# The run-up to the first pass of a two-layer decoder trunk: c spread over partitions another way, x in four transfers, the first weights in three pieces

## The chip, the cores and the metric

One core of a Trainium2 chip runs the kernel. The metric is the device time of one execution in microseconds (us), the median over runs.

## What is computed

A trunk of two decoder layers over 256 tokens of width 1024, all in float32. Each layer has a token mixer (layer 0: dilated windowed attention; layer 1: gated linear attention) and a gated convolutional feed-forward part. Each of these four sub-layers is fed a normalised and modulated x; shift, scale and gate come from a conditioning vector c:

```python
mod = jax.nn.silu(c) @ w_ada[i] + b_ada[i]                 # c: (1, 1024), w_ada[i]: (1024, 6*1024)
sh1, sc1, g1, sh2, sc2, g2 = split(mod, 6)
h = rmsnorm(x, norm_mix[i]) * (1.0 + sc1) + sh1            # x: (1, 256, 1024)
y = dilated_mixture(h, w_in_a, w_out_a, rel_bias)          # layer 0; begins with h @ w_in_a
x = x + g1 * y
...
```

`rmsnorm(x, g)` is x / sqrt(mean(x*x) + eps) * g, the mean over the 1024 features.

## The kernel before

x is held transposed: `x_all` is 128 partitions by 8 tiles (`kt`) by 256 tokens, so that a tile `kt` holds 128 of the 1024 features. Products keep float32 accuracy by splitting both operands in a high part (`hi`, in the fp32r format) and a low part (`lo`, what is left): a product is hi*hi + hi*lo + lo*hi.

What lies ahead of the first pass, and the lines that matter:

- **c.** A DMA on ScalarE's queue (line 84) brings c into one partition of `c_row`. Two products with a stationary operand of one row (line 123) spread it over all 128 partitions, ScalarE's Silu (line 124) turns it into `c_bc`. Two more DMAs on that queue bring `small` (biases and norms), `tab` and `oh` (the relative bias table and a one-hot matrix).
- **x.** Two DMAs on SyncE's queue (SP, line 90), 512 KB each.
- **The mean square.** VectorE squares tiles 0 to 3 in one instruction (line 385), ScalarE squares 4 to 7 in two (line 388); VectorE adds each half down to one tile in two sums (line 391); two products with a matrix of 1/1024 (line 211, in `rstd_of`) sum over partitions; Ln and Exp (lines 213 and 215) make `rstd`.
- **Filling products.** `keep_warm` (line 297) issues products whose result nobody reads: 4 behind the products of c, 3 behind the mean square, 6 behind the rows of the bias (line 405), which are themselves three small products of `oh` and `tab`.
- **The first pass**, a loop over the 8 tiles `kt`. For each tile SP loads 1 MB of modulation weights (`ada_load`, line 133) and 960 KB of attention weights (`split`, line 166). VectorE takes two dot products of 1024 columns with `c_bc` (`ada_dot`, line 140); ScalarE adds bias and factor (lines 148 and 150); VectorE forms `xr` (line 283), ScalarE its high part `hhi` (line 285), VectorE the low part `hlo` (line 287). The weight tile is cast to its high part `whi` in two halves of 960 columns on ScalarE (line 172), the low parts `wlo` are VectorE's (line 184). TensorE then multiplies (lines 675 and 679, and 199 to 201 for the rest). For kt = 0 both loads go in two DMAs.

The order of the instructions of an engine follows from a scheduler, with dependences written out by hand: `behind(a, b)` and `issue_after` put an instruction behind others. The weights' raw buffers are four in number (`wraw`), so a load waits until the tile two rounds back has been consumed. Each DMA of SP and ScalarE also waits for the DMA eight places ahead of it among those of these two queues.

## Time and profile before

| | |
|---|---|
| time, median of 3 runs | 765.04 us (764.12 to 766.68) |
| the profiled execution: time, span | 764.38 us, 762.6 us |
| TensorE busy, VectorE, ScalarE, GpSimd | 754.2, 649.4, 486.2, 33.6 us of the span |
| granted TensorE clock | 1.00 |
| HBM read | 184.43 MB, 243 GB/s over the span |

The page gives busy times, the span in slices, the chain of work that ended last, and groups of instructions. A row of the timeline has the start in us from the span's start, the duration, the engine, the line and operation, what it writes and reads, and in brackets how long the engine had been idle and what ended that. "PE" is TensorE, "PEld" its weight loads, "DVE" VectorE, "ACT" ScalarE, "SPq" and "ACTq" the instruction queues that issue DMAs. A row of DMA issues has the number of issues, their size and the median time from issue to landing. A row of the windows has the stretch, its length, the busy time of the five engines (with instructions started), the granted clock, the share of time in which the 16 DMA engines were busy, and GB/s.

### The profile page before, as it was taken

Reading aid. Unit: us, or ns where it says so; the run is one execution under the profiler, and the core shown is the slowest. Engines: PE = TensorE matmul, PEld = TensorE weight load, DVE = VectorE, ACT = ScalarE, POOL = GpSimd, SP = SyncE. Lnnn points to the kernel's source line nnn. Section 1 sums busy time; section 2 is a strip of 40 time slices with the busy share of each in tenths; the row PEclk is TensorE's granted clock in tenths of the full one; section 3 lists DMA queues with packets and bytes.
Section 4 is the critical chain, followed back from the end, with each engine's and each line's share of the span. In section 5 each row is a group of like instructions: output and inputs, shape, how many; then the busy total and the mean of one; then the engine's idle time right before and its main releaser. Section 6 shows DMA issues by size and latency. Waiting matters only on the chain.

```text
span 762.6 us, 16024 instructions
## 1 busy us (share of the span) xinstructions
PE 754.2 (99%) x6394; PEld 731.5 (96%) x6394; DVE 649.4 (85%) x1185; ACT 486.2 (64%) x951; POOL 33.6 (4%) x56
## 2 busy tenths in 40 slices
PE   8999999999999999999999999999999999999997
PEld 6999999999999999999999998899999999999997
DVE  6997999898989678999999778797668999998592
ACT  6476676565566478776777456746766866666551
POOL 0001101101101010000000000000010000000100
PEclk9999999999999999999999999999999999999999
DMA  9988889778787357878556976875356777774631
GB/s 348 404 287 312 318 293 325 281 256 307 285 275 254 112 198 257 319 262 277 202 172 234 340 263 228 305 275 178 132 190 216 241 269 271 209 174 157 200 104 56
DMA packets 39225, 186.57 MB, mean 245 GB/s; under 512 B 9004, under 2 KB 11820, under 8 KB 25070
## 3 DMA queue, kind: packets, MB, share of 16 engines
q1 hardware_dynamic: 38768, 185.10, 69.6%
q8 instruction: 50, 0.82, 0.4%
q10 hardware_dynamic: 382, 0.45, 0.2%
q14 instruction: 25, 0.20, 0.1%
HBM read 184.43 MB, written 1.10 MB: 243 GB/s over the span
## 4 chain that ended last, share of the span: by engine, by line
PE 94%; DVE 3%; DMA 2%; issue 1%; ACT 0%; DVEq 0%; ACTq 0%
PE pab L199 10%; PE pab L200 10%; PE pab L201 10%; PE pqk L199 5%; PE pd L199 5%; PE pd L200 5%; PE pd L201 5%; PE pqk L201 5%; PE pqk L200 5%; PE pv L199 3%; PE pv L200 3%; PE pv L201 3%; PE pqk L675 2%; PE py L199 2%; PE py L201 2%; PE py L200 2%
## 5 line engine op out<-in xcount | busy, mean ns | idle before, releaser
L172 ACT CAST whi<-raw 128x1024 fp32r<-128x1024 f32 (+4 forms) x262 | 237.7, 951 | 92.6 <-PE pab L200 35.5
L178 DVE TENSOR_TENSOR wlo<-raw,whi 128x1024 fp32r<-128x1024 f32 (+3 forms) x246 | 263.8, 1097 | 38.5 <-ACT whi L172 37.5
L200 PE MATMUL pab<-hlo,whi 128*128 128x256 f32 x672 | 184.6, 276 | 0.0
L201 PE MATMUL pab<-hhi,wlo 128*128 128x256 f32 x672 | 184.6, 276 | 0.0
L199 PE MATMUL pab<-hhi,whi 128*128 128x256 f32 x672 | 183.2, 277 | 0.0
L200 PEld LDWEIGHTS pab<-hlo,whi 128*128 128x128 f32 x672 | 126.0, 188 | 0.2
L201 PEld LDWEIGHTS pab<-hhi,wlo 128*128 128x128 f32 x672 | 126.1, 188 | 0.0
L199 PEld LDWEIGHTS pab<-hhi,whi 128*128 128x128 f32 x672 | 125.1, 188 | 0.1
L140 DVE CUSTOM_DVE_ANT_0 ada_raw<-ada_raw,c_bc 128x1024 f32<-128x1024 f32 x96 | 114.1, 1229 | 4.7 <-DMA ada_raw<-in_w_ada 4.7
L199 PE MATMUL pqk<-hhi,whi 128*128 128x256 f32 x356 | 98.0, 281 | 0.0
L200 PE MATMUL pqk<-hlo,whi 128*128 128x256 f32 x356 | 97.4, 279 | 0.0
L201 PE MATMUL pqk<-hhi,wlo 128*128 128x256 f32 x356 | 96.8, 279 | 0.2 <-DVE wlo L178 0.2
L200 PE MATMUL pd<-glo,whi 128*128 128x256 f32 x308 | 84.8, 276 | 0.0
L201 PE MATMUL pd<-ghi,wlo 128*128 128x256 f32 x308 | 84.8, 276 | 0.0
L199 PE MATMUL pd<-ghi,whi 128*128 128x256 f32 x308 | 84.7, 276 | 0.0
L201 PEld LDWEIGHTS pqk<-hhi,wlo 128*128 128x128 f32 x356 | 65.9, 188 | 1.1 <-issue 0.7
L200 PEld LDWEIGHTS pqk<-hlo,whi 128*128 128x128 f32 x356 | 66.7, 188 | 0.1
L199 PEld LDWEIGHTS pqk<-hhi,whi 128*128 128x128 f32 x356 | 66.5, 188 | 0.1
L200 PEld LDWEIGHTS pd<-glo,whi 128*128 128x128 f32 x308 | 57.7, 188 | 0.0
L201 PEld LDWEIGHTS pd<-ghi,wlo 128*128 128x128 f32 x308 | 57.7, 188 | 0.0
L199 PEld LDWEIGHTS pd<-ghi,whi 128*128 128x128 f32 x308 | 57.7, 188 | 0.0
L962 ACT ACTIVATE r<-pab,small 128x256 f32<-128x256 f32 x86 | 47.5, 561 | 7.0 <-DVE r L965 6.7
(269 smaller groups left out, 1498.8 us busy)
## 6 DMA issues: line engine op xcount, KB each, us to landing
raw<-in_w_up SPq DMA_DIRECT2D x42, 1024.0 KB, 4.9
ada_raw<-in_w_ada SPq DMA_DIRECT2D x29, 1024.0 KB, 5.8
raw<-in_w_down SPq DMA_DIRECT2D x28, 704.0 KB, 4.3
ada_raw<-in_w_ada SPq DMA_DIRECT2D x38, 512.0 KB, 6.8
raw<-in_wqk SPq DMA_DIRECT2D x18, 1024.0 KB, 6.9
raw<-in_wv SPq DMA_DIRECT2D x14, 768.0 KB, 6.5
raw<-in_w SPq DMA_DIRECT2D x7, 960.0 KB, 6.5
raw<-in_w_out_a SPq DMA_DIRECT2D x4, 1024.0 KB, 6.9
```

Source lines behind the costliest of these rows:

```text
L140: i = nc.vector.tensor_tensor_reduce(w, w, c_bc, op0=ALU.mult, op1=ALU.add, scale=1.0, scalar=0.0, accum_out=dot,)
L172: copied[0] = nc.scalar.copy(hi[:, c], raw[:, c])
L178: last_lo[0] = nc.vector.tensor_tensor(lo[:, c], raw[:, c], hi[:, c].bitcast(F32), op=ALU.subtract)
L199: mm(ps, a[0], b[0], start=start, stop=False)
L200: mm(ps, a[0], b[1], start=False, stop=False)
L201: return mm(ps, a[1], b[0], start=False, stop=stop)
L675: mm(pqk[i], w[a], h[kt][b], start=s and i % 2 == 0 and (a, b) == (0, 0), stop=e and i % 2 == 1 and b == 1)
L962: nc.scalar.activation(r, u[:, :T], AF.Identity, scale=cw[2], bias=col(C_CB + 44 * l + f))
```

## The change

- c is brought into partitions 0, 32, 64 and 96 of `c_row`, a quarter of it (256 columns) each, behind a VectorE memset of those 256 columns and behind the DMA of `small` on ScalarE's queue. Four products of 128 rows, each with a stationary matrix that holds 1/1024 in the one row that it picks and zero elsewhere (`chosen`, set by GpSimd), spread it.
- Three filling products stand ahead of those of c; the 4 behind c and the 3 behind the mean square are gone, and the 6 behind the bias rows become 2.
- x comes in four DMAs of 256 KB.
- VectorE squares tiles 0 to 3 and 6 to 7 in three instructions, ScalarE 4 to 5; one sum for each half leaves two tiles, and the mean square takes four products in place of two. The two Silus of c are ordered around ScalarE's square.
- `tab` and `oh` move from ScalarE's queue to SP's, behind the first modulation weights.
- The first weight tile comes in three DMAs of 512, 448 and 960 columns, and its casts and low parts go in the same three pieces. The first modulation scale is computed on VectorE instead of ScalarE.
- For kt = 1 to 5 the order of TensorE's products within a tile differs: those with `hlo` stand ahead of those of line 679 (now 743), as they do for kt = 6 and 7 in both kernels. Behind the first pass all engines have the same instructions in the same order.

```diff
     c_row = wspl.tile([P, 2048], F32, tag="whi", name="c_row")
-    nc.scalar.dma_start(c_row[:1, :D], I["c"])
+    chosen = c_row[:, 512:1024].rearrange("p (i m) -> p i m", i=4)
+    nc.vector.memset(c_row[:, 0:T], 0.0)
+    ones_d = const.tile([P, P], F32, name="ones_d")
+    nc.vector.memset(ones_d, 1.0 / D)
+    nc.gpsimd.memset(chosen, 0.0)
+    for i in range(4):
+        nc.gpsimd.memset(chosen[32 * i : 32 * i + 1, i, :], 1.0 / D)
+    small = const.tile([P, C_END], F32, name="small")
+    nc.scalar.dma_start(small[:, :C_CW], I["small"][:, :C_CW])
+    nc.scalar.dma_start(c_row[0:P:32, 0:T], I["c"].rearrange("o (a b) -> (o a) b", a=4))
...
-    for i in range(2):
-        nc.sync.dma_start(x_all[:, 4 * i : 4 * i + 4, :], I["xR"][:, 4 * i : 4 * i + 4, :])
+    for i in range(4):
+        nc.sync.dma_start(x_all[:, 2 * i : 2 * i + 2, :], I["xR"][:, 2 * i : 2 * i + 2, :])
...
+    last_c = keep_warm(3)
     c_bc = const.tile([P, D], F32, name="c_bc")
-    for n in range(2):
-        ps = bank("cb", "t")
-        last_c = mm(ps, ones_d[:1, :], c_row[:1, 512 * n : 512 * n + 512], start=True, stop=True)
-        silu = nc.scalar.activation(c_bc[:, 512 * n : 512 * n + 512], ps, AF.Silu, scale=float(D))
+    c_ps = [bank("cb", "t") for _ in range(2)]
+    for i in range(4):
+        with behind(last_c):
+            last_c = mm(c_ps[i // 2][:, T * (i % 2) : T * (i % 2) + T], chosen[:, i, :], c_row[:, 0:T], start=True, stop=True)
...
-    with behind(last_c):
-        keep_warm(4)
-    nc.vector.tensor_tensor(sq[:, 0:4, :], x_all[:, 0:4, :], x_all[:, 0:4, :], op=ALU.mult)
-    with behind(silu):
-        for i in (4, 6):
-            last_sq = nc.scalar.activation(sq[:, i : i + 2, :], x_all[:, i : i + 2, :], AF.Square)
-    for n in (0, 4):
-        for m in (2, 1):
-            last_add = nc.vector.tensor_tensor(sq[:, n : n + m, :], sq[:, n : n + m, :], sq[:, n + m : n + 2 * m, :], op=ALU.add)
...
-    r = rstd_of([sq[:, 0, :], sq[:, 4, :]])
+    last = square(0)
+    with behind(last):
+        last = square(2)
+    with behind(silu_of(0)):
+        last_sq = nc.scalar.activation(sq[:, 4:6, :], x_all[:, 4:6, :], AF.Square)
+    with behind(last):
+        last = add(0)
+    with behind(last_sq):
+        silu = silu_of(1)
+    exp_ln_after(silu)
+    with behind(last):
+        last = square(6)
+    with behind(last):
+        last = add(4)
+    with behind(last):
+        last = scale_terms(0)
+    r = rstd_of([sq[:, i, :] for i in (0, 1, 4, 5)])
+
+    first_ada = ada_load(0, 0, 2)
+    nc.sync.dma_start(tab[:32, :], I["rel_bias"])
+    nc.sync.dma_start(oh[:33, :NROW], I["onehot"])
...
     with behind(last_row):
-        keep_warm(6)
+        keep_warm(2)
...
+    CUTS = (0, 512, 960, 1920)
...
+    def first_tile(last):
+        with behind(last):
+            dots = [ada_dot(0, 0, 0, first_ada, on_vector=True)]
+        raw = wraw.tile([P, 2048], F32, tag="raw", name="raw")
+        for a, b in zip(CUTS, CUTS[1:]):
+            last_load[0] = nc.sync.dma_start(raw[:, a:b], I["w0"][0][:, a:b])
...
+        with behind(norm_ops[1]):
+            cast = piece(w, 0, 0)
+        with behind(dots[0][1], cast):
+            dots.append(ada_dot(0, 0, 1, first_ada))
+
+        def between(scaled, high):
+            with behind(scaled):
+                j = piece(w, 0, 1)
+            with behind(high):
+                i = piece(w, 1, 0)
+            with behind(i):
+                copied[0] = piece(w, 2, 0)
+            return [j]
...
```

More of the change, by code (lines that the diff above doesn't have):

```diff
@@ L76, in trunk, with behind @@
     mm = nc.tensor.matmul
+    @contextmanager
+    def behind(*those):
+        with ExitStack() as st:
+            for i in those:
+                st.enter_context(tc.issue_after(i.ins))
+            yield
     def exp_ln_after(last):
@@ L268, in trunk @@
     squared = [None, None]
-    @contextmanager
-    def behind(*those):
-        with ExitStack() as st:
-            for i in those:
-                st.enter_context(tc.issue_after(i.ins))
-            yield
     def normed(l, sub, r, kt, first=(), between=None):
@@ L407, in trunk, with piece @@
     with behind(last_row):
-        keep_warm(6)
+        keep_warm(2)
     w0, h = [], []
-    last = last_add
-    for kt in range(KT):
-        ada = ada_load(0, kt, 1 if kt else 2)
-        with behind(*((last,) if kt else (norm_ops[1], last))):
+    CUTS = (0, 512, 960, 1920)
+    def piece(w, i, op):
+        c = slice(CUTS[i], CUTS[i + 1])
+        hi, lo, raw, _ = w
+        if op:
+            return nc.vector.tensor_tensor(lo[:, c], raw[:, c], hi[:, c].bitcast(F32), op=ALU.subtract)
+        return nc.scalar.copy(hi[:, c], raw[:, c])
+    def first_tile(last):
[4 more added lines that the diff above has]
+            last_load[0] = nc.sync.dma_start(raw[:, a:b], I["w0"][0][:, a:b])
+        hi = wspl.tile([P, 2048], F32R, tag="whi", name="whi")
+        lo = wspl.tile([P, 2048], F32R, tag="wlo", name="wlo")
+        w = hi, lo, raw, 960
+        w0.append(w)
+        with behind(norm_ops[1]):
[10 more added lines that the diff above has]
+            return [j]
+        with behind(dots[1][1]):
+            h.append(normed(0, 0, r, 0, (dots[1][0],), between))
+        last = chain[0][1]
+        for i in (1, 2):
+            with behind(last):
+                last = piece(w, i, 1)
+        return last
+    last = first_tile(last)
+    with behind(copied[0]):
+        for ps, c in rows_ps:
+            nc.scalar.copy(rows[:, c], ps)
+    for kt in range(1, KT):
+        ada = ada_load(0, kt)
+        with behind(last):
             dots = [ada_dot(0, kt, 0, ada)]
@@ L429, in trunk @@
             last = low_part(w0[kt], 1)
-        if kt == 0:
-            with behind(copied[0]):
-                for ps, c in rows_ps:
-                    nc.scalar.copy(rows[:, c], ps)
         if kt == 1:
```

39 lines of the change are left out of this document (20 added, 19 removed).

## The prediction

> **What bounds the kernel now.** I read the page first, then the chain of waits, then the timeline of the first 60 us engine by engine, then the DMA rows. The page's head:
>
> ```profile
> span 762.6 us, 16024 instructions
> ...
> PE 94%; DVE 3%; DMA 2%; issue 1%; ACT 0%; DVEq 0%; ACTq 0%
> ```
>
> TensorE owns the chain, and all that the change touches lies ahead of its first real product. The chain, in order of time (start, us, what):
>
> ```profile
> 0.74 1.37 DMA c_row<-in_c
> ...
> 2.24 3.76 PE cb L123 x4
> ...
> 8.90 1.22 PE ms L211 x2
> ...
> 11.33 1.40 PE rows L405 x6
> 12.72 1.53 PE warm L297 x12
> 14.26 1.42 PE pqk L675 x12
> ...
> 46.04 2.33 PE pqk L675 x18
> ...
> 51.54 1.76 PE pqk L675 x14
> ...
> 278.32 1.29 PE ms L211 x6
> ```
>
> The first pass (line 675, eight tiles kt = 0 to 7) starts at 14.26, right behind six filling products. It looks as if everything follows from that start. It does not; the timeline of VectorE and ScalarE shows who sets the pace later:
>
> ```profile
> 8.76 1.22 DVE L140 CUSTOM_DVE_ANT_0 ada_raw<-ada_raw,c_bc 128x1024 f32<-128x1024 f32 x1
> ...
> 11.39 0.48 DVE L283 SCALAR_TENSOR_TENSOR xr<-x_all,mod,rstd 128x256 f32<-128x256 f32 x1 [0.26 <-ACT mod L148]
> ...
> 15.00 1.22 DVE L140 CUSTOM_DVE_ANT_0 ada_raw<-ada_raw,c_bc 128x1024 f32<-128x1024 f32 x1
> ...
> 16.75 1.00 ACT L172 CAST whi<-raw 128x960 fp32r<-128x960 f32 x1
> ...
> 17.79 1.16 DVE L184 TENSOR_TENSOR wlo<-raw,whi 128x960 fp32r<-128x960 f32 x1
> ...
> 20.58 1.22 DVE L140 CUSTOM_DVE_ANT_0 ada_raw<-ada_raw,c_bc 128x1024 f32<-128x1024 f32 x1
> ...
> 25.95 1.22 DVE L140 CUSTOM_DVE_ANT_0 ada_raw<-ada_raw,c_bc 128x1024 f32<-128x1024 f32 x1
> ...
> 45.47 0.51 ACT L285 ACTIVATE hhi<-xr,mod 128x256 fp32r<-128x256 f32 x1 [0.36 <-ACT mod L150]
> ...
> 50.84 0.51 ACT L285 ACTIVATE hhi<-xr,mod 128x256 fp32r<-128x256 f32 x1
> ```
>
> VectorE begins kt = 1 at 15.00, kt = 2 at 20.58, kt = 3 at 25.95: 5.37 us a tile. TensorE needs (46.04 - 14.26) / 6 = 5.30. So TensorE's lead melts, and by kt = 6 it is gone: hhi is ready at 45.98 and the products start at 46.04; for kt = 7 at 51.35 and 51.54. The end of the pass is VectorE's as much as TensorE's. A TensorE that starts earlier alone gains nothing; VectorE's start of kt = 2 must move.
>
> What holds that? The cast of the second weight tile w1 at 16.75; the low part at 17.79 follows it. The DMA answer for the issue at 6.80, the DMA stream (last three columns: clock, share of the engines busy, GB/s), and the issue itself:
>
> ```profile
> 6.80 0.56 SPq L166 DMA_DIRECT2D raw<-in_w  x1
> ...
> raw<-in_w SPq DMA_DIRECT2D x1, 960.0 KB, 9.9
> ...
> 2.00:4.00 2.00, 1.76 (x2) 0.83 (x3) 0.00 (x0) 1.28 (x1) 0.00 (x0) 1.00 0.81 256
> 4.00:8.00 4.00, 4.00 (x12) 2.42 (x11) 2.73 (x5) 2.56 (x5) 0.00 (x0) 1.00 0.98 353
> 8.00:12.00 4.00, 3.95 (x12) 2.35 (x12) 3.58 (x7) 2.77 (x6) 0.00 (x0) 1.00 1.05 420
> 12.00:17.00 5.00, 5.00 (x40) 4.63 (x39) 4.54 (x6) 3.14 (x8) 0.00 (x0) 1.00 1.00 415
> ```
>
> w1 lands at 6.80 + 9.9 = 16.7, and ScalarE casts it at 16.75. It isn't late by its issue: the DMA engines are full from 4 us on. Moved by 17.0: 2 x 256 + 4 x 353 + 4 x 420 + 5 x 415 = 5.68 MB; wanted up to w1: x, two modulation tiles and two weight tiles, small, table and one-hot, 5.3 MB, reached at 16.1. So w1 comes when the stream has carried what stands ahead of it.
>
> **The change part by part.** Times are of the profiled execution: 764.38 us, of which 762.6 are span. It lies 0.66 under the median 765.04, on which I state the forecast.
>
> ```profile
> 0.74 0.86 SPq L90 DMA_DIRECT2D x_all<-in_xR  x2
> 1.65 1.31 SPq L133 DMA_DIRECT2D ada_raw<-in_w_ada  x2
> 3.01 2.32 SPq L166 DMA_DIRECT2D raw<-in_w  x2
> ...
> x_all<-in_xR SPq DMA_DIRECT2D x1, 512.0 KB, 4.2
> ...
> x_all<-in_xR SPq DMA_DIRECT2D x1, 512.0 KB, 5.2
> ...
> small<-in_small ACTq DMA_DIRECT2D x1, 71.0 KB, 5.3
> ...
> tab<-in_rel_bias ACTq DMA_DIRECT2D x1, 6.0 KB, 6.4
> ...
> ada_raw<-in_w_ada SPq DMA_DIRECT2D x1, 512.0 KB, 6.5
> ...
> raw<-in_w SPq DMA_DIRECT2D x2, 480.0 KB, 6.9
> ...
> 6.02 0.60 ACT L124 ACTIVATE c_bc<-cb 128x512 f32<-128x512 f32 x1 [1.11 <-PE cb L123]
> ...
> L391 DVE TENSOR_TENSOR sq<-sq 128x512 f32<-128x512 f32 x2 | 1.4, 692 | 0.2 <-ACT sq L388 0.2
> ...
> 10.66 0.42 ACT L215 ACTIVATE rstd<-ln 128x256 f32<-128x256 f32 x1
> ...
> out_y<-y SPq DMA_DIRECT2D x2, 256.0 KB, 2.1
> ```
>
> *x in quarters, squares and sums.* The halves landed 4.2 and 5.2 us after issues at 0.74 and about 1.2: at 4.9 and 6.4. Quarters by interpolation: 3.9, 4.9, 5.7, 6.4. VectorE then has three squares, two sums, each 0.69, and scale_terms: 3.9, 4.9 to 5.6, sum to 6.3, square of the last quarter 6.4 to 7.1, sum to 7.8, terms to 8.0. The two sums of 256 columns go to TensorE as two more products.
>
> *c.* It now waits for a VectorE memset (0.3 us) and stands behind small on ScalarE's queue; behind it wait the table load and both Silus. Before it took 1.37 us, alone. The nearest row for a transfer behind small is tab: 6.4 us; small itself: 5.3. But those ran beside 1 MB of x in 4 KB rows; here small leaves first, beside a quarter. Between 2.5 and 6.6 us I take 3.7, nearer the first row since small no longer queues behind x. Products: four of 256 columns, 1024 as before, 3.76 us at the slow rate, so to 7.5; Silus 0.6 each, the second to 8.2. The first dot starts at 8.2 instead of 8.76 (its weights land at 1.65 + 6.5 = 8.15).
>
> *Mean square.* Four products in place of two. Slow rate: 3.76 x 256 / 1024 = 0.94 each; fast: 1.29 / 3 = 0.43. The rows of 1024 columns in 3.76 and of 768 columns in 1.40 (line 405) show TensorE doubling its rate between 6 and 11 us. Behind c at 7.5: end 9.2 if fast at once, 11.3 if slow throughout; I take 9.9. Ln and Exp ended 0.96 after the products (10.12 to 10.66 + 0.42); so rstd at 10.9, against 11.08. The fillings ahead of c are there for that rate: three at the front, two instead of nine behind. The Trainium skill (TensorE: Matmul & The Clock Gate, Part 1) says that the clock doubles after a busy window of some 3.4 us that runs free of the kernel's start; by that rule the end lies between 9.2 and 11.3 by chance, and the granted clock in the profile's rows, 1.00 throughout, can't show it.
>
> *First weights in three pieces.* The last 960 columns land where w0's second half did: issued by 5.0, about 6.9 later, 11.9. Cast 0.98, low part 1.16. With rstd at 10.9, xr (0.48) ends at 11.4, hhi (0.51) at 11.9; ScalarE then casts 448 and 960 columns, by the row of 1.00 for 960 to 13.4, and VectorE's last low part ends, and kt = 1 begins, at 14.5 instead of 15.00 (14.05 if only the weights hold it, 15.9 if TensorE stays slow). TensorE's first product starts near 12.0 instead of 14.26.
>
> *SP's queue.* Table and one-hot move onto it, and each issue waits for an earlier transfer: tab for small, one-hot and the pieces for quarters of x and c, w1 for the first modulation half (8.15; before 6.80). Behind these stands the whole weight stream; but by the sums above the stream reaches w1 only near 13.7, so this costs nothing unless small takes past 7 us. Bytes ahead of w1 are the same. The two 100 KB transfers no longer interleave from another queue: by the rows 4 to 8, 353 against 420 GB/s, up to 0.3 us could come back. x in 2 KB rows could lose: in its first 2 us the stream made only 256 GB/s in 4 KB rows. At half that, +2 us; at the writes' rate (two output transfers of 256 KB in 2 KB rows, 2.1 us to land) nothing. I take zero, nearest to the output row. The Trainium skill (DMA: Bandwidth & Descriptors, Rules for kernel authors) speaks against this edit: at least 1 MiB per transfer for full rate. The trace bears it out no further than that a 512 KB half took 4.2 us.
>
> *Sum.* Before kt = 1: -0.5. There it is given back: w1 still lands at 16.7, its cast ends at 17.75, and VectorE, ready two dots and xr after 14.5, at 17.4, waits. Low part, hlo, low part again end at 20.5, as before. From there 5.37 a tile, unchanged instructions. Net -0.1, bounds -0.4 (stream 0.3 earlier) and +0.9 (kt = 1 at 15.9). Later stages have the same instructions in the same order, and shift with the pass.
>
> **The rivals.** *TensorE sets it:* the earlier start carries through, -2.3 us, 762.7. For it: the chain names TensorE from 14.26 on. Against: the ties at 45.98 and 51.35, and w1 at 16.7; it needs w1 by 14.5, with the stream at 420 GB/s from its first byte. *c late:* c lands behind small. Up to 4.2 us it is free (kt = 1 then begins at 15.0); beyond, each us of c is a us of Silu, dot and pass. At small's old landing (1.3 + 5.3 = 6.6): +2.4, less 0.3 for products already fast, 767.1. For it: the tab row. Against: small leaves first. *x slow in small rows:* the stream, and w1 with it, between 0 and 2 us later, 1 us in the middle: 766.0; decided by whether 256 GB/s is a rate per byte or per row. *The fillings don't bring the fast rate:* kt = 1 at 15.9, +0.9, 765.9: the upper end of the main range, and part of its chance.
>
> **How the numbers follow.** Main case 0.70, 764.9, own range 764.6 to 765.9. TensorE's pace 0.08, c late 0.10, slow x 0.12. A measurement here can tell about 0.3%, 2.3 us: under 762.7 or over 767.3. The first takes half of TensorE's case and some scatter (three runs spread 2.6 us): 0.07. The second takes half of c late and some scatter: 0.07. The range that holds 8 in 10: 763.2 to 766.8.
>
> **What would show it.** Right: VectorE's first dot near 8.2, kt = 1 near 14.5, TensorE's first product near 12 but with waits for hhi ahead of kt = 1 to 7 that it did not have; w1's cast still at 16.7 to 16.8; kt = 2 at 20.5. Wrong: w1 cast before 16.0 (then the stream was faster), kt = 2 under 19.5, or c's first product after 4.2.

## The result and the profile after

The changed kernel takes 765.75 us (median of 22 runs, 765.14 to 767.16); the kernel before, beside it on the same chip, 764.59 us (22 runs, 763.65 to 766.68). The ratio is 1.0015, 95% interval 1.0009 to 1.0022: slower by 0.7 to 1.7 us where I had forecast 0.1 us faster. It is half of the 0.3% that I had called the limit of measurement, yet the interval excludes no change, and the traces show what the run-up and the first pass lose. The profiled execution took 765.36 us, of which 763.6 are span (before: 764.38 and 762.6).

The chain of waits of the changed kernel, its first 21 us (start, us, what):

```profile
0.74 3.71 DMA small<-in_small
...
4.46 0.34 SPq L420
...
4.85 0.50 SPq L421
...
5.40 0.36 SPq L451
...
7.27 8.75 DMA ada_raw<-in_w_ada
...
16.05 1.23 DVE ada_raw L162
...
18.46 0.02 ACT mod L175
...
18.66 0.98 ACT whi L197
...
19.67 1.16 DVE wlo L209
```

Before, TensorE owned the chain from c onwards. Now the chain runs through SP's queue: `small` has to land before SP issues the table (line 420) and the one-hot matrix (421), behind these stand the three pieces of w0 (451), behind these the modulation weights of kt = 1, and on them hangs VectorE's kt = 1. TensorE has dropped out of it. Its rows:

```profile
4.69 3.75 PE L143 MATMUL cb<-c_row 128*128 128x256 f32 x8 [1.72 <-DMA c_row<-in_c]
8.23 2.04 PE L236 MATMUL ms<-sq,ones_d 128*128 128x256 f32 x8
...
13.31 0.72 PE L739 MATMUL pqk<-hhi,whi 128*128 128x256 f32 x4
...
20.10 0.97 PE L739 MATMUL pqk<-hhi,whi 128*128 128x256 f32 x6 [1.28 <-ACT hhi L302]
...
52.64 0.97 PE L739 MATMUL pqk<-hhi,whi 128*128 128x256 f32 x6
...
58.53 0.44 PE L224 MATMUL pv<-whi,hhi 128*128 128x384 f32 x1 [0.24 <-ACT v L688]
```

TensorE does start earlier (13.31; the same row of the timeline of before reads 14.02), runs through kt = 0, and then stands for 1.28 us at kt = 1, waiting for hhi. The rows of before for kt = 1 and 7, and the end of kt = 1's hhi on ScalarE, which stand in no fence so far:

```profile
17.98 0.51 ACT L285 ACTIVATE hhi<-xr,mod 128x256 fp32r<-128x256 f32 x1
...
19.39 0.87 PE L675 MATMUL pqk<-hhi,whi 128*128 128x256 f32 x6
...
51.40 0.97 PE L675 MATMUL pqk<-hhi,whi 128*128 128x256 f32 x6
...
57.30 0.44 PE L199 MATMUL pv<-whi,hhi 128*128 128x384 f32 x1 [0.28 <-ACT v L624]
```

None of the products of the pass waits there. And on TensorE nothing waits in the changed kernel either between the hole at kt = 1 and `pv`, so the changed order of its products costs no idle time. The next stage's first product (`pv`, the last row) is my mark for the end of the pass; it moves by 58.53 - 57.30 = +1.23 us. That this comes so near the loss in time (+1.16) is in part chance, for later stages give some of it back. The first product `pab` of the next sub-layer, before and after, is only 0.57 us late:

```profile
281.87 0.58 PE L199 MATMUL pab<-hhi,whi 128*128 128x256 f32 x2
```

```profile
282.44 0.47 PE L224 MATMUL pab<-hhi,whi 128*128 128x256 f32 x1
```

The spans of these two executions differ by 1.0; the rest of that arises near the end, where both kernels have the same instructions. So the sections below explain the 1.23 us of the pass; how much of the microsecond in time each part makes is not shown. What made hhi late in the changed kernel, on VectorE and ScalarE:

```profile
9.27 1.23 DVE L162 CUSTOM_DVE_ANT_0 ada_raw<-ada_raw,c_bc 128x1024 f32<-128x1024 f32 x1 [0.58 <-DMA ada_raw<-in_w_ada]
...
11.90 0.48 DVE L300 SCALAR_TENSOR_TENSOR xr<-x_all,mod,rstd 128x256 f32<-128x256 f32 x1
...
14.58 1.16 DVE L443 TENSOR_TENSOR wlo<-raw,whi 128x960 fp32r<-128x960 f32 x1 [0.35 <-ACT whi L444]
16.05 1.23 DVE L162 CUSTOM_DVE_ANT_0 ada_raw<-ada_raw,c_bc 128x1024 f32<-128x1024 f32 x1 [0.31 <-DMA ada_raw<-in_w_ada]
...
22.30 1.21 DVE L162 CUSTOM_DVE_ANT_0 ada_raw<-ada_raw,c_bc 128x1024 f32<-128x1024 f32 x1
...
18.46 0.29 ACT L175 ACTIVATE mod<-dot,small 128x1 f32<-128x1 f32 x1 [0.76 <-DVE dot L162]
18.66 0.97 ACT L197 CAST whi<-raw 128x960 fp32r<-128x960 f32 x1
19.54 0.50 ACT L302 ACTIVATE hhi<-xr,mod 128x256 fp32r<-128x256 f32 x1
```

hhi of kt = 1 ends at 20.04, before at 18.49: +1.55. It adds up from three rows. The first dot waits for its weights: 9.27 instead of 8.76, +0.51. From the first dot to xr it takes 2.63 us in both. From xr to the first dot of kt = 1 it takes 4.15 instead of 3.61, +0.54, with waits of 0.35 for the third cast and 0.31 for the next modulation weights. And on ScalarE w1's cast now stands between the second mod and hhi (before it stood between the two mods): from xr to the end of hhi 1.70 instead of 1.20, +0.50. w1 itself lands 1.6 us later too (below), but in this order its cast could not have run before the second mod anyway. Why the weights are late, SP's issues and the stream (last three columns: clock, share of the DMA engines busy, GB/s):

```profile
0.74 1.82 SPq L107 DMA_DIRECT2D x_all<-in_xR  x4
2.60 0.91 SPq L155 DMA_DIRECT2D ada_raw<-in_w_ada  x2
4.46 0.34 SPq L420 DMA_DIRECT2D tab<-in_rel_bias  x1
4.85 0.50 SPq L421 DMA_DIRECT2D oh<-in_onehot  x1
5.40 1.83 SPq L451 DMA_DIRECT2D raw<-in_w  x3
7.27 0.49 SPq L155 DMA_DIRECT2D ada_raw<-in_w_ada  x1
9.14 0.33 SPq L191 DMA_DIRECT2D raw<-in_w  x1
```

```profile
4.00:8.00 4.00, 3.31 (x8) 2.72 (x9) 2.81 (x5) 1.12 (x2) 0.00 (x0) 1.00 0.93 306
8.00:12.00 4.00, 2.80 (x12) 1.83 (x11) 3.39 (x8) 3.01 (x5) 0.00 (x0) 1.00 1.05 356
12.00:17.00 5.00, 5.00 (x39) 4.43 (x37) 4.27 (x6) 3.31 (x8) 0.00 (x0) 1.00 1.02 422
```

Four issues of x take 1.82 us where two took 0.86, so the first modulation weights are issued 0.95 later, at 2.60 (1.65 before). Behind them stand the table's wait for `small` (3.50 to 4.46) and the issues of table and one-hot: w0 is issued at 5.40 (3.01), w1 at 9.14 (6.80). The stream carries 306 instead of 353 GB/s from 4 to 8 us and 356 instead of 420 from 8 to 12: 4 x 47 + 4 x 64 = 0.44 MB less, about a microsecond at 420. From 8 to 12 the DMA engines are as busy as before (1.05 in both), so there they do not lack work: the same busy time moves fewer bytes. The modulation weights of kt = 1 land at 16.0; w1, with 9.2 us from issue to landing, at 18.3 instead of 16.7.

### The profile page after: what moved, and what is told of

It is laid out like the page before. It is cut to its first block, busy times and chain, and to the rows that moved or that the text cites. A ratio compares the mean times of both kernels' runs of the same rounds, so it can differ in the third digit from the quotient of the medians.

```text
span 763.6 us, 16024 instructions
## 1 busy us (share of the span) xinstructions
PE 752.5 (99%) x6386; PEld 731.5 (96%) x6386; DVE 650.2 (85%) x1188; ACT 485.6 (64%) x950; POOL 34.8 (5%) x61
## 4 chain that ended last, share of the span: by engine, by line
PE 90%; DVE 5%; ACT 2%; DMA 2%; issue 1%; SPq 0%; DVEq 0%; ACTq 0%
PE pab L225 10%; PE pab L226 10%; PE pab L224 10%; PE pd L226 5%; PE pd L225 5%; PE pd L224 5%; PE pqk L224 5%; PE pqk L226 5%; PE pqk L225 5%; PE pv L224 4%; PE pv L225 4%; PE pv L226 4%; PE py L224 2%; PE py L226 2%; PE py L225 2%; DVE ada_raw L162 2%
## 5 line engine op out<-in xcount | busy, mean ns | idle before, releaser
L197 ACT CAST whi<-raw 128x1024 fp32r<-128x1024 f32 (+3 forms) x260 | 235.6, 950 | 90.7 <-PE pab L225 35.3
```

Of the source, the lines that this page charges most:

```text
L197: copied[0] = nc.scalar.copy(hi[:, c], raw[:, c])
```

## The experiments

Main theory after the result ("transfers"): the loss comes from how the changed transfers are issued. Rivals: c is late; ScalarE's order costs it; the changed arithmetic ahead of kt = 1 costs it. Each kernel was timed in five rounds beside the kernel before. The intervals are about 0.8 us to each side, wider than most of the disputed terms, so these are read from the timeline (one execution each), and the table has both. A timeline has its own scatter: with the same transfers ahead of it, the first dot starts at 9.17 (e13) to 9.99 (e14), so differences of half a microsecond between two rows prove little. "First dot", "kt = 1", "kt = 2" are VectorE's starts, "cast" is the first cast of w1, "mark" the next stage's first product; all in us.

| kernel | median (before) | ratio, 95% | first dot | kt = 1 | cast | kt = 2 | mark |
|---|---|---|---|---|---|---|---|
| before | | | 8.76 | 15.00 | 16.75 | 20.58 | 57.30 |
| changed | 765.75 (764.59) | 1.0009 to 1.0022 | 9.27 | 16.05 | 18.66 | 22.30 | 58.53 |
| e4 | 766.47 (764.50) | 1.0004 to 1.0032 | 10.47 | 17.05 | 19.65 | 23.29 | 59.45 |
| e1 | 765.96 (764.50) | 1.0004 to 1.0024 | 10.95 | 17.10 | 18.65 | 22.55 | 58.72 |
| e5 | 765.90 (764.50) | 1.0001 to 1.0025 | 9.57 | 16.20 | 18.81 | 22.44 | 58.59 |
| e2 | 765.43 (764.50) | 0.9995 to 1.0016 | 9.77 | 16.28 | 18.89 | 22.52 | 59.53 |
| e9 | 765.39 (764.77) | 0.9998 to 1.0021 | 9.63 | 16.42 | 18.12 | 21.95 | 58.86 |
| e10 | 766.99 (764.77) | 1.0018 to 1.0038 | 9.47 | 15.97 | 18.38 | 22.19 | 59.41 |
| e13 | 766.18 (764.77) | 1.0009 to 1.0036 | 9.17 | 15.32 | 17.93 | 21.57 | 58.82 |
| e14 | 764.42 (764.77) | 0.9986 to 1.0009 | 9.99 | 16.14 | 17.70 | 21.60 | 58.17 |
| e6 | 766.44 (764.78) | 1.0018 to 1.0037 | 9.64 | 15.88 | 17.69 | 21.50 | 60.73 |
| e17 | 765.93 (764.78) | 1.0004 to 1.0025 | 9.58 | 16.64 | 19.05 | 22.86 | 59.04 |
| e18 | 770.73 (764.78) | 1.0069 to 1.0101 | 9.42 | 16.24 | 18.64 | | 58.54 |
| e20 | 765.34 (764.99) | 0.9979 to 1.0007 | 8.40 | 16.50 | 18.05 | 21.95 | 58.45 |
| e22 | 765.69 (764.99) | 0.9983 to 1.0010 | 8.99 | 16.33 | 18.27 | 22.08 | 58.26 |
| e21 | 766.13 (764.99) | 0.9992 to 1.0018 | 8.91 | 16.07 | 18.32 | 22.12 | 58.63 |
| e24 | 765.50 (764.99) | 0.9983 to 1.0011 | 8.73 | 16.16 | 17.72 | 21.63 | 58.13 |
| e26 | 765.63 (764.48) | 1.0000 to 1.0022 | 9.64 | 16.11 | 18.51 | 22.33 | 58.49 |
| e27 | 765.03 (764.48) | 0.9990 to 1.0013 | 9.63 | 16.13 | 18.42 | 22.23 | 58.93 |

The runs of before beside e20 to e24 spread up to 768.3, so that the ratios there lie lower than the medians suggest. In several kernels (e2, e9, e13, e14, e20, e21, e24, e27) TensorE waits 0.2 to 0.7 us more at later tiles, and in e6 and e10 it is slow at the start, so that their mark says less than their kt = 2.

### Transfers put back one by one: e4, e1, e5, e2

e4 puts the order and the sizes of the transfers back but keeps c on four partitions; e1 puts back x in two; e5 issues c ahead of `small`; e2 loads w0 in two.

```diff
 e1, e4: -for i in range(4): nc.sync.dma_start(x_all[:, 2*i : 2*i+2, :], ...)
         +for i in range(2): nc.sync.dma_start(x_all[:, 4*i : 4*i+4, :], ...)
 e4, e5: c's transfer ahead of small's; e4: table and one-hot behind it on ScalarE's queue
 e2, e4: -for a, b in zip(CUTS, CUTS[1:]):
         +for a, b in ((0, 960), (960, 1920)):
```

> The changed kernel with the transfers of before: x in two, the first weights in two, table and one-hot on ScalarE's queue, c ahead of small. All arithmetic, the fillings and the three casts stay as changed. Theory of the stream (the transfers now carry the same bytes later, w1 lands later, and kt = 2 follows w1): w1 is cast at 16.7 to 16.9 as before the change, kt = 2 begins at 20.5, time within 0.3 us of the kernel before, while TensorE's first product stays early, near 12. Rival (the arithmetic of the run-up costs it: more products, more pieces, c later): kt = 2 stays at 21.5 or later, time 0.8 to 1.2 us above before.

> The changed kernel with x in two transfers of 4 KB rows again, the rest as changed. Theory of the stream, with the 2 KB rows of x as its cause: w1 cast near 17.2 instead of 18.66, kt = 2 near 21, time 0.3 to 0.5 us above before instead of 1.2. If x's rows are not the cause: kt = 2 at 22.0 to 22.3, 1.0 to 1.2 above before. Rival (c behind small): c lands no earlier beside larger rows, 1.2 or more above before.

> The changed kernel with the transfer of c issued ahead of that of small, the rest as changed. Theory of the stream: c lands near 2.7 and its products run 2 us earlier, but the first dot waits for its weights at 9.1 to 9.3, w1 is cast at 18.5 to 18.7, kt = 2 at 22.2, and the time stays 1.0 to 1.3 us above before. Rival (c late is what costs it): first dot near 8.3, kt = 2 near 21, time 0 to 0.4 above before.

> The changed kernel with the first weight tile in two transfers of 960 columns; its casts and low parts stay in three pieces. Theory of the stream, if the rows of 2 KB and 1.8 KB of the pieces cost it what the windows from 9 to 11 us lost: w1 cast near 18.2, kt = 2 near 21.9, time 0.8 us above before. If the pieces cost nothing: kt = 2 at 22.3, 1.2 above before.

None brought the microsecond back (in time, of these four only e2 cannot be told from before, and not from the changed kernel either), and kt = 2 came later in e4 and e1 than in the changed kernel. The reason is c: it waits for a memset, is issued at about 1.2, and so stands behind x. With x in halves its first product came at 6.05 (e4) and 6.53 (e1) instead of 4.69, and the first dot waited for Silu, not for weights. Both runs traded one delay for another, and their kt = 2 cannot tell the theories apart. The landings can: with x in two, the first modulation weights of e1 were issued at 1.66 and landed 6.2 us later, at 7.9 (changed: 2.60 and 6.5, at 9.1), and w1 at 7.87 + 9.4 = 17.3 (changed 18.3). So x in four does delay the weights, by about a microsecond, and c, as brought here, holds the first dot even without that. e5 shows that `small` ahead of c is not what delays it (first product 5.47). e2 shows that the third transfer of w0 is not the cause (kt = 2 at 22.52).

### ScalarE's order: e9

The second mod of kt = 1 is put behind w1's first cast, as it ran before.

```diff
+held = (nc.scalar.copy(hi[:, :960], raw[:, :960]),)     # kt == 1 only
+dots.append(ada_dot(0, kt, 1, ada, held=held))          # its mod goes behind(held)
```

> The changed kernel, with ScalarE's order at kt = 1 put back to mod, cast, mod (in the changed kernel it is mod, mod, cast). Theory 'weights' (w1's landing sets kt = 2): w1 still lands near 18.3 us, its cast starts at 18.4 instead of 18.66, kt = 2 starts near 22.1 instead of 22.30, and the time moves by no more than -0.2 us against the changed kernel, so about 1.0 us over before. Rival 'order' (the cast queued behind the second mod costs the 0.7 us by which the step from kt = 1 to kt = 2 has grown): kt = 2 near 21.6, time 0.5 us over before.

kt = 1 began later here (16.42), yet kt = 2 earlier (21.95): the step is 5.53 us instead of 6.25. The cast starts at 18.12, just behind w1's landing, and hhi ends at 19.86. So the order costs the step 0.7 us, of which 0.35 arrive at kt = 2. Of the two texts, the rival's mechanism is shown and the main theory's "no more than 0.2" falls; the time (+0.6) fits the rival but its interval holds both. All later kernels on the changed one but e10 and e13 have this order forced; in e10, as in e1, the scheduler chose it by itself.

### c as before: e10

```diff
-nc.scalar.dma_start(c_row[0:P:32, 0:T], I["c"]...)      # behind small and a memset
+nc.scalar.dma_start(c_row[:1, :D], I["c"])              # first on the queue, one row
```

> The changed kernel, with c loaded and spread as before: one row, first on ScalarE's queue, with no memset ahead, and two products of 512 columns; all else (small second, x in quarters, fillings ahead, sums on TensorE, weights in pieces, table on SP's queue) as changed. Theory 'weights': c lands near 2.1, the second Silu ends near 8.2, but the first dot still waits for the modulation weights at about 9.1 and w1 still lands about 18.3, so kt = 2 starts at 22.0 to 22.3 and the time is 1.0 to 1.3 us over before. Rival 'c late': the first dot moves to about 8.3, kt = 1 to about 15.1, kt = 2 to about 20.7, and the time comes within 0.3 us of before.

c came early (first product 2.63, second Silu over at 7.43), and the first dot still waited 0.94 for its weights: 9.47. So c alone does not hold the first dot of the changed kernel. Still, c is a near second: the second Silu ends at 9.07 in the changed kernel, and in e9, with the same transfers, at 9.60, so that there the first dot waited for c. "c late" is hidden by the weights, not refuted. The time of e10 was the worst of these, for a reason that neither text had: the sums of the mean square.

```profile
6.83 3.78 PE L231 MATMUL ms<-sq,ones_d 128*128 128x256 f32 x8 [0.43 <-DVE sq L394]
```

3.78 instead of 2.04 us for the same four products, and TensorE stayed at this slow rate into the pass (first four products of kt = 0 in 1.20 instead of 0.72). More of it at e26.

### Table left out, and 1 MB left out: e13, e14

```diff
 e13: -nc.sync.dma_start(tab[:32, :], ...); nc.sync.dma_start(oh[:33, :NROW], ...)
      +nc.gpsimd.memset(tab[:32, :], 0.0); nc.gpsimd.memset(oh[:33, :NROW], 0.0)
 e14: no load of the modulation weights of kt = 1; its dots multiply x instead; order as e9
```

> The changed kernel, leaving out the loads of the bias table and the one-hot matrix (both filled with zeros by GpSimd instead, so the bias rows are not those of the reference; the products of them stay). It takes 105 KB and two issues, one of which waits for small, out of SP's queue ahead of the weights. Theory 'table on SP': the two transfers and the wait for small are what slows the stream between 5 and 11 us; then w1 lands near 17.2 instead of 18.34, kt = 2 starts near 21.1 and the time is about 0.2 us over before. Theory 'small rows' (quarters of x in 2 KB rows and pieces of w0 in 1.8 to 3.8 KB rows slow the stream): only the 105 KB go, 0.25 us; w1 near 18.1, kt = 2 near 22.0, the time 1.0 us over before.

> The changed kernel, with the 1 MB of modulation weights for kt = 1 left out of the stream (its two dots read x instead, so the modulation of kt = 1 is not the reference's; VectorE's work is the same) and ScalarE's order at kt = 1 put to mod, cast, mod. Theory 'weights': w1 lands 2.4 us sooner, near 15.9, no longer holds anything; kt = 1 starts at about 15.7 (held by the run-up alone), kt = 2 at about 21.2, and the time is about 0.7 us over before: the run-up on VectorE alone is 0.7 us slower than before, and the rest of the loss is the stream. Rival 'run-up' (the stream does not matter, the work on VectorE and ScalarE ahead of kt = 2 does): kt = 2 stays near 22, the time 1.1 us over before.

e13, in stretches of one microsecond; the changed kernel carried 314 and 308 GB/s in the same two:

```profile
9.00:10.00 1.00, 1.00 (x6) 0.61 (x4) 0.83 (x1) 0.98 (x2) 0.00 (x0) 1.00 1.04 391
10.00:11.00 1.00, 1.00 (x4) 0.29 (x4) 0.96 (x4) 0.96 (x3) 0.00 (x0) 1.00 1.05 422
```

The trough goes with the table; kt = 1 begins at 15.32 with no wait, w1's cast directly behind the mods at 17.93. So table and one-hot are part of the loss, and not by their 105 KB alone: 0.19 MB more in these two microseconds. kt = 2 came 0.7 us earlier, halfway between the two texts (21.1 and 22.0), but the time did not follow: at 45.23 a cast waited 0.53 for weights, and the mark is 58.82. In e14 the weights hold nothing at kt = 1 or kt = 2 (cast at 17.70, no wait), and kt = 1 still starts at 16.14: the first dot waited 1.13 for the first modulation weights. kt = 2, at 21.60, lies between its two texts (21.2 and 22) as well, and only 0.35 ahead of e9, which has the same order and the load. Its time equals that of before, although its mark lies 0.9 us behind; later stages give most of that back (its first `pab` at 282.06, 0.19 behind). Both show the stream ahead of kt = 2 as a cost, and e14 that the run-up's own delay, here, comes mostly from the first modulation weights.

### Issues or small rows: e6, e21, e17

e6 is the kernel before with x in four and nothing else. e21 is the kernel before with two transfers of 32 bytes behind x. e17 is the changed kernel with table and one-hot on ScalarE's queue, order as e9.

```diff
 e6:  +for i in range(4): nc.sync.dma_start(x_all[:, 2*i : 2*i+2, :], ...)     # 2 KB rows
 e21: +for i in range(2): nc.sync.dma_start(extra[i : i+1, :], I["c"][:, 8*i : 8*i+8])
 e17: -nc.sync.dma_start(tab ...), nc.sync.dma_start(oh ...)
      +nc.scalar.dma_start(tab ...), nc.scalar.dma_start(oh ...)
```

> The kernel before, with x in four transfers instead of two; nothing else. Theory 'small rows' (x in 2 KB rows slows the stream by 0.15 MB between 4 and 7 us): w1 lands near 17.1 instead of 16.7, kt = 2 starts near 20.9 instead of 20.58, the first product of the next stage comes near 57.6 instead of 57.30, the time is 0.3 us over before. Rival 'rows do not matter' (my prediction's zero): w1 within 0.15 us of 16.75, kt = 2 within 0.15 us of 20.58, the time unchanged.

> The kernel before with two more transfers on SP's queue right behind x, of 32 bytes each, whose data nobody uses; x stays in two transfers with 4 KB rows. Theory 'issues' (each issue takes SP 0.45 us, and all that stands behind it starts that much later): the first modulation load is issued near 2.6 instead of 1.65, w1 lands 0.7 to 1.0 us later, cast near 17.5, kt = 2 near 21.4, time 0.7 to 1.2 us over before, as with x in four (1.66). Rival 'small rows' (the 2 KB rows of x in four are what slowed the stream): w1 within 0.2 us of 16.75, kt = 2 within 0.2 us of 20.58, time within 0.3 us of before.

> The changed kernel, with table and one-hot issued on ScalarE's queue behind small and c, as before, instead of on SP's queue ahead of the weights, and ScalarE's order at kt = 1 put to mod, cast, mod. Theory 'place' (it is the place in SP's queue, with its wait for small, that costs): the trough of 308 to 314 GB/s at 9 to 11 us goes, kt = 1 starts near 15.4, w1 is cast by 17.3, kt = 2 starts near 20.9, the first product of the next stage near 57.6, time 0.2 to 0.3 us over before. Rival 'transfer' (the 33 rows of 3 KB cost the stream half a microsecond wherever they run): the trough only moves to 6 to 8 us, kt = 1 near 16, kt = 2 near 21.6 (the gain of the order alone), time 0.6 to 0.8 us over before.

SP's issues and w1's cast in e6:

```profile
0.74 1.82 SPq L90 DMA_DIRECT2D x_all<-in_xR  x4
2.60 1.81 SPq L133 DMA_DIRECT2D ada_raw<-in_w_ada  x2
5.63 0.93 SPq L166 DMA_DIRECT2D raw<-in_w  x2
...
17.69 0.99 ACT L172 CAST whi<-raw 128x960 fp32r<-128x960 f32 x1 [0.17 <-DMA raw<-in_w]
```

and in e21:

```profile
1.66 0.65 SPq L93 DMA_DIRECT2D extra<-in_c  x2
2.35 2.96 SPq L136 DMA_DIRECT2D ada_raw<-in_w_ada  x2
6.65 0.81 SPq L169 DMA_DIRECT2D raw<-in_w  x2
...
18.32 0.99 ACT L175 CAST whi<-raw 128x960 fp32r<-128x960 f32 x1 [0.60 <-DMA raw<-in_w]
```

x in four alone puts w1 about 0.95 us later, more than half of what the whole change does (and more than its text had for small rows), and the time 1.4 to 2.8 us up. (Its mark of 60.73, and so part of its time, has a further cause: TensorE stayed at its slow rate, and kt = 0's first product came only at 17.46.) Two idle transfers of 32 bytes do more still to w1 (+1.6), while x keeps its rows of 4 KB; in time, e21 cannot be told from before. So the number of transfers is enough to make w1 late. That the length of x's rows adds nothing is not shown: from 2 to 4 us e6 carried 235 GB/s at a busy share of 0.89, the kernel before 256 at 0.81. The rows show two parts: each issue takes SP about 0.45 us, and a later issue stands until an earlier transfer has landed (the two modulation issues take 2.96 us in e21, 1.81 in e6, 1.31 before, 0.91 in the changed kernel, which stands at its next issue instead). Which one it waits for, SP's waits tell: the transfer eight places ahead, counted over both queues. In e21 (who waited for whom: us in all, times, longest):

```profile
SPq L136 <- DMA x_all<-in_xR: 2.2, 1, 2.2
SPq L169 <- DMA x_all<-in_xR: 1.3, 1, 1.3
```

and in the changed kernel:

```profile
SPq L191 <- DMA ada_raw<-in_w_ada: 1.4, 1, 1.4
SPq L420 <- DMA small<-in_small: 0.9, 1, 0.9
```

Before, the second modulation load is issued at 2.12 without a wait, and w0's second half is the first to wait for x (until 5.00). Two more transfers, of whatever size, move these waits up by two places: in e21 the second modulation load is issued at 4.96, when x's first half has landed, and w0 at 6.65 instead of 3.01, when the second has. Of these 3.6 us the two issues themselves take 0.65. The DMA engines ran dry meanwhile: busy share 0.60 and 156 GB/s from 4 to 5 us in e6, 0.53 and 187 from 9 to 10 in e21. e17 shows that another queue is no way out: SP then stands from 2.56 to 4.17 before it issues the first modulation weights, and w1's cast waits 0.74 for its weights until 19.05. Its kt = 2, at 22.86, is later than in either of its texts.

The Trainium skill (DMA: Bandwidth & Descriptors, "Issuing engines are not separate DMA queues") says that starting transfers from several engines saves only the starting time, usually small beside the transfer. The first half agrees with e17, and an issue of 0.45 us is small beside the 4 to 10 us from issue to landing. What counts here is how many stand ahead of w0, eight where there were four, and what each of them waits for.

### Who sets the pace: e18

```diff
+skip = l == 0 and 1 <= n < KT and s == 1     # the second dot of tiles 1 to 7 is left out
```

> The changed kernel with the second dot (1.22 us on VectorE) of each tile kt = 1 to 7 left out, so the shifts of these tiles are not the reference's; ScalarE's order at kt = 1 is mod, cast, mod. VectorE then needs 4.15 us a tile. Theory 'VectorE paces the pass': TensorE, at 5.30 a tile, sets the end: kt = 0's products start near 13.3, kt = 1's wait for w1 (18.3 + 1.0) until 19.4, and the next stage's first product comes at about 57.0 instead of 58.53; the time falls by 1.4 us against the changed kernel. Rival 'TensorE paces it already': the next stage's first product stays at 58.4 to 58.6.

> The kernel before with the same dots left out (the shifts of tiles 1 to 7 are not the reference's). Theory 'VectorE paces the pass': TensorE starts at 14.26 and runs 8 x 5.30 without a wait, so the next stage's first product comes near 57.0 instead of 57.30 (0.3 us, the two paces being nearly tied); against the changed kernel without the dots it comes at the same time within 0.4 us, so that TensorE's start, 0.95 us earlier in the changed kernel, is lost to w1 even with VectorE out of the way. Rival: were TensorE's start all that matters, this kernel would be 0.95 us slower than the changed one without the dots.

TensorE at kt = 1 and kt = 7 in e18:

```profile
20.42 0.97 PE L762 MATMUL pqk<-hhi,whi 128*128 128x256 f32 x6 [1.47 <-ACT hhi L310]
...
52.20 0.92 PE L762 MATMUL pqk<-hhi,whi 128*128 128x256 f32 x6
```

With 1.22 us less on VectorE per tile, TensorE runs at its own 5.30 us from kt = 1 to kt = 7 ((52.20 - 20.42) / 6); in the changed kernel it takes (52.64 - 20.10) / 6 = 5.42. So VectorE does pace the later tiles, but that is worth (5.42 - 5.30) x 6 = 0.7 us; the hole at kt = 1 is there without it too. The forecast of 57.0 was missed: the mark stayed at 58.54, the number of the rival, as hhi of kt = 1 came at 20.37, not at 19.4, and `pv` waited 0.65 for v. The times (770.73; e19 772.61, 1.0095 to 1.0122) say nothing of this question: e19's scheduler put seven mods ahead of Silu on ScalarE, so that the first dot started at 12.53, and e18 too runs in another order behind the pass. e19 is not used.

### All transfers back, and what arithmetic remains: e20, e22, e24

```diff
 e20: x in two, c in one row and first, table on ScalarE's queue, w0 in two; fillings as before,
      with the three ahead of c; sums, mod, three casts as changed; order as e9
 e22: as e20, but table on SP's queue and w0 in three
 e24: as e20, and w1 in two transfers
```

> The changed kernel with every transfer as before: x in two, c as one row first on ScalarE's queue (so the two one-row products, with four fillings behind them and three ahead of the bias rows as before), small, table and one-hot behind it, w0 in two. The changed arithmetic stays: fillings ahead of c, sums on TensorE, mod of kt = 0 on VectorE, casts and low parts of w0 in three; ScalarE's order at kt = 1 is mod, cast, mod. Theory 'transfers': w1 is cast by 16.9 us again, kt = 1 starts near 15.0, hhi of kt = 1 ends by 18.6, TensorE has no hole at kt = 1, the first product of the next stage comes at 57.1 to 57.5, the time is within 0.3 us of before. Rival 'arithmetic' (three casts and low parts and the mod on VectorE cost the run-up half a microsecond or more): kt = 1 at 15.6 or later, the next stage's first product near 57.9, time 0.5 us over before.

> As the run before (e20), but table and one-hot stay on SP's queue ahead of the weights and w0 in three pieces, as changed: only x (in two) and c (one row, first) are put back. Theory 'issues on SP': three more issues of 0.4 to 0.5 us, one of them waiting, ahead of the weights put w0 and w1 about 1 us later than in e20: w1 cast near 17.7, kt = 1 near 15.6, the next stage's first product near 58.0, time 0.6 to 0.8 us over before. Rival 'x alone' (all of the loss is x in four): as e20 within 0.2 us.

> e20 with w1 loaded in two halves, so that its first cast can start before all of w1 is there. If kt = 1 starts near 14.8 and w1's first half lands near 15.8, VectorE's step to kt = 2 is 5.4 us with no wait: kt = 2 near 20.2, the next stage's first product 0.2 to 0.4 us ahead of 57.30, time 0.2 to 0.4 us under before. If instead the casts were not held by w1 in e20, or the further issue costs its 0.45 us again, it is the same as e20 or up to 0.3 us slower.

In e20 the first dot is early (8.40) and xr is late all the same:

```profile
8.21 3.62 PE L237 MATMUL ms<-sq,ones_d 128*128 128x256 f32 x8
...
12.82 0.48 DVE L301 SCALAR_TENSOR_TENSOR xr<-x_all,mod,rstd 128x256 f32<-128x256 f32 x1 [1.74 <-ACT rstd L241]
```

The four sums ran at the slow rate again, and rstd held xr until 12.82 (11.39 before). In the timeline the main text is wrong, and the rival right only in its number: kt = 1 at 16.50 is "15.6 or later", but for a cause outside the arithmetic that it names. In time, e20 is indistinguishable from before (0.9979 to 1.0007), and so are e22 and e24. e22's first dot and kt = 2 lie 0.6 and 0.1 us behind e20's; its w1 landed at 18.2, in e20 at 17.0, and the stream carried 349 GB/s from 8 to 12 us (402 in e20). So table and pieces on SP's queue make w1 late with x in two as well: "x alone" falls, and the parts do not simply add up. e24 lies 0.3 us ahead of e20 from xr on (12.49), but by its sums (3.06 us); w1's halves gained nothing, since in e20 no weights held the cast either. No version here beats the kernel before, and none has the transfers of before together with fast sums, so that the two could be weighed against each other.

### Fillings or full height, and two pieces: e26, e27

```diff
 e26: -last_c = keep_warm(3)                 # order as e9
 e27: -CUTS = (0, 512, 960, 1920)            # order as e9
      +CUTS = (0, 960, 1920)
```

> The changed kernel without the three filling products ahead of c; ScalarE's order at kt = 1 is mod, cast, mod. Theory 'full height' (products that use all 128 rows bring TensorE to its fast rate, one-row products do not): c's products still take 3.4 to 3.8 us and the four sums behind them 1.9 to 2.1 us, as in the changed kernel; kt = 1 near 16.0 to 16.4, time as e9 (0.6 us over before) within 0.3 us. Rival 'fillings' (it is the three products at the front that start the change of rate): the sums take 3.6 us, rstd and xr come 1.2 us or more later, near 13.1, kt = 1 near 17.2, time 1.5 us over before.

> The changed kernel with w0 in two transfers, two casts and two low parts as before; ScalarE's order at kt = 1 is mod, cast, mod. Theory 'pieces cost VectorE' (three low parts with waits between take longer than two): from xr of kt = 0 to the first dot of kt = 1 it takes 3.6 to 3.8 us instead of 4.15, kt = 1 starts near 15.6, and TensorE's first product comes 0.4 us later than 13.31, at about 13.7, with no hole at kt = 1 or one under 0.5 us; time 0.3 to 0.5 us over before. Rival 'stream alone' (kt = 1 is held by its modulation weights at 16.0): kt = 1 stays at 16.0 to 16.4, time 0.6 us or more over before.

e26's sums:

```profile
8.30 1.93 PE L237 MATMUL ms<-sq,ones_d 128*128 128x256 f32 x8
```

Without the three fillings ahead of c the sums are as fast as with them, so the fillings at the front do nothing that shows; with one-row products of c (e20, e10) the sums are slow. Over all kernels with four sums, those with full-height c took 1.89 to 2.99 us, those with one row 3.06 to 3.78. The lengths of single products tell when the rate doubles: 3.3 to 5.9 us after the first product of 128 rows in a run of such (from 4.69 to 8.59 in the changed kernel, 5.21 to 11.15 in e9, 5.94 to 9.53 in e21, 6.34 to 11.83 in e20), whether one-row products stood ahead of it or not. With the full-height c this run begins sooner (4.69 in the changed kernel, 5.92 before). Why it takes 3.3 us in one kernel and 5.9 in another was not followed. In e6 and e10, where TensorE pauses between the sums and what follows, the fast rate came only at 19 to 20 us. The Trainium skill (TensorE: Matmul & The Clock Gate, Part 1) has the clock double after a window of some 3.4 us in which TensorE is busy. From c's first product (4.69) to the first fast sum (8.59) this fits; but in e20 TensorE is busy with one-row products from 2.63 on and still slow at 11.2, 8.6 us later, so products of one row do not seem to count. The granted clock reads 1.00 throughout and shows none of it.

e27 saves TensorE nothing at the start (14.18, for the first cast is longer), and kt = 1 stays at 16.13; from xr to it 3.86 us instead of 4.15. The time is the closest to before among the kernels that keep x in four (0.9990 to 1.0013), but its interval overlaps that of e26, which has three pieces. That three pieces cost is not shown.

## Why the prediction was wrong

- **VectorE's start of kt = 2 decides, not TensorE's start: right.** TensorE starts 0.7 us earlier and loses it, and more, in one hole of 1.28 us at kt = 1. "VectorE paces the pass" was too strong: the hole is hhi of kt = 1, late by weights and order; the pace behind it adds 0.7 us (e18).
- **SP's queue, "this costs nothing unless small takes past 7 us": the step that failed.** `small` landed at 4.45, and the chain still runs through it. I had named the waits and then priced them at nothing, by the mean rate of the stream, as if bytes were always waiting. They were not: with more transfers ahead, the waits leave the DMA engines short of work (busy share 0.60 in e6, 0.53 in e21, for a microsecond each), and the stream carried 306 GB/s from 4 to 8 us where I had reckoned with 353. From 8 to 12, where it carried 356 for 420, the engines were busy all the same; there the table and one-hot cost the stream (414 without them, e13). Everything behind landed later: w0's last piece at 13.5 where I had 11.9, the modulation weights of kt = 1 at 16.0 (14.4 before), w1 at 18.3 where I had kept 16.7.
- **x in quarters, "I take zero": failed, by the wrong question.** I weighed the price of 2 KB rows (0 to 2 us) and not the two issues more, which stood in a row that I quoted: 0.86 us for two. e6 puts the price near 0.95 us at w1, and e21 shows that issues and their waits are enough for it. The rival "x slow in small rows" had about the right time (766.0) for a reason that no run separates out: luck, as far as this shows.
- **First dot at 8.2: failed** by the same omission. The weights' landing was kept at 8.15 although their issue moves from 1.65 to 2.60; they landed at 9.1, and the dot came at 9.27.
- **c at 3.7, free up to 4.2: missed** (first product 4.69), at no cost in the changed kernel, because the weights are later still: the second Silu ends at 9.07, the first dot waits until 9.27 (and in e10 until 9.47 with c long there). But the 0.2 us between them are all that hides it: had the weights landed at 8.15, the first dot would have waited for c until 9.1, so "c late" is no more than covered.
- **The sums, 9.9: close** (10.27), in part by luck: c's products ended 0.9 late, and the sums took 2.0 us where I had 2.4. The doubt about the fast rate was the right one; full-height products of c bring it sooner, the fillings that I gave it to do not (e26).
- **kt = 1 at 14.5: 16.05.** Of the 1.55, 1.0 is xr, which starts at 11.90 for 10.9, and comes from the first dot. The other 0.55 lie between xr and kt = 1 (4.15 us for 3.6), where VectorE waits 0.35 for the third cast and 0.31 for the next modulation weights.
- **Cast of w1 at 16.75 between the two mods: missed.** The changed kernel runs mod, mod, cast, hhi. That order could be read before the run, and I took the old one. It costs the step 0.7 us (e9).
- **kt = 2 at 20.5: 22.30.** The test I had named for "wrong", c's first product after 4.2, did fire, for a delay that the weights covered.

What stays open: why a table of 105 KB costs the stream 0.19 MB more than its bytes, why some kernels wait 0.2 to 0.7 us at later tiles, and how much of the 1.23 us at the mark is left in the time when later stages have given some of it back.

## What to carry to other kernels

Where a stage waits for a stream of loads, count the transfers ahead of it and what each issue waits for, before the bytes: in a kernel where each transfer waits for the one eight places ahead, two transfers of 32 bytes made w1 later than cutting 1 MB in four did. A mean rate proves a load free only if the queue never runs dry and what stands ahead runs at that rate, so look at the share of busy DMA engines and at the GB/s in stretches of a microsecond. And an edit that starts one engine earlier is worth what the next wait leaves of it: name that wait, and read the new order of every engine around it, not only of the one that the edit is about.

## What the runs showed of the hardware that I had not expected

- An issue on SP's queue took 0.33 to 0.46 us in most cases, and up to 1.18 (the one-hot matrix in e22). The 2.96 for two in e21 is 0.36 and 0.35 of issue and 2.2 of waiting for x's first half.
- Products of one row did not bring TensorE to its fast rate: in e20 they ran from 2.63 to 6.4 us, and the rate doubled at 11.8, 5.5 us after the first product of 128 rows behind them. The four sums took 3.06 to 3.78 us behind one-row products, 1.89 to 2.99 behind products of 128 rows, at a granted clock of 1.00 in both.
- A transfer of 4 KB issued 0.4 us behind the first of x lands 2 to 4 us later than one issued with it: c's first product at 2.24 before, at 4.69 to 6.53 in the kernels that issue it at 1.2. These kernels bring it as four rows, not one, so that place and form are not told apart. (Its issue also takes longer, 1.1 us for four rows against 0.5 for one.)
